# Four instead of three seven-product couples in nine of eleven gate-and-up groups, two low parts a group on GpSimd

## The chip, the cores and the metric

One core of one Trainium2 chip runs the whole program; the other cores are idle. The metric is the device time of one execution in microseconds (us). The median of the runs is compared. A smaller number is better.

## The reference

A two-layer decoder trunk over 256 tokens with a model width of 2048 and a hidden width of 5632. Layer 0 is a Conformer convolution, layer 1 a dilated attention; each is followed by a SwiGLU block. Only the two SwiGLU blocks matter here:

```python
def _swiglu(h, w_gate, w_up, w_down):
    return (jax.nn.silu(h @ w_gate) * (h @ w_up)) @ w_down
...
    for layer in range(DEPTH):
        ...                                   # convolution (layer 0) or attention (layer 1)
        h = h + _swiglu(_rmsnorm(h, ffn_norm_g[layer]), ffn_w_gate[layer],
                        ffn_w_up[layer], ffn_w_down[layer])
    return _rmsnorm(h, final_norm_g)
```

All inputs and outputs are float32.

## The kernel before

**Products.** TensorE multiplies in a rounded 32-bit form (fp32r). To keep float32 accuracy each operand is split in a high part (the value copied into fp32r) and a low part (the value minus its high part). A product of two operands is three matmuls: high by high, high by low, low by high (`nat`, lines 409, 411, 414). Activations are split once; weights are split as they arrive. A weight block is 2 x 128 rows by 512 columns, 128x1024 elements on chip. It is loaded by a DMA of SyncE's queue into a `raw` buffer (3 of them), ScalarE copies it into `whi`, VectorE subtracts into `wlo` (`split`). `whi` and `wlo` have four buffers each, and `next_block` keeps the emission two blocks ahead of the block that TensorE uses, so that a block can be prepared while TensorE is at most four blocks behind.

**Gate and up.** `ffn_hidden` runs once in each layer. It goes over 11 groups `c`; a group makes 512 gate columns and 512 up columns for all 256 tokens (two halves of 128). The 2048 input rows are 8 couples of 2 x 128 rows. A plain couple ("n" in the items string) takes one gate block and one up block, 12 matmuls of 128x512 each, together 24. A couple by seven products ("S") treats tokens x rows and rows x (gate, up) as 2 x 2 matrices and needs 7 instead of 8 products, 21 matmuls (`seven`). For that it needs sums of the activation parts, made once (`sum_up`, kept in `xsums`), and four sums of weight parts: `emit_sums` loads the four parts into one tile `four` (two DMAs of GpSimd's queue, `load_sums`), and prepares four "quarters" q = 0 to 3 with one 1024-element low part each (512 at q = 1), and with three more subtractions `less` on VectorE (line 261). Group 0 has plain couples only (the sums are made beside it); groups 1 to 10 have `"nnSnSnSn"`: two plain couples ahead, then S and n in turn.

**End of a group.** After the last S `combine_into` (line 569, 571) puts the seven products' four extra PSUM banks together: one ScalarE copy and four VectorE additions into `work`. `hidden` then adds the group's own banks (line 713), ScalarE makes the silu (717), VectorE multiplies gate and up (724). A few block steps later `turned` transposes the result on TensorE (736), and ScalarE and VectorE split it into `hid` (738, 739). PSUM has eight banks: the four that hold one group's sums of products (`cs`) are the extra banks (`ps`) of the next, and the other way round, so a group's first matmuls wait until the additions of `combine_into` have read the banks, and the first S of a group waits for the last readers of the previous group's `cs`.

**Order.** Each engine works off its own queue in order. A scheduler orders instructions; `in_order` pins a chosen sequence of those on one engine. `later(n, ...)` runs a piece of work after n + 1 block steps (`tick`).

Lines 229 to 276 (splitting and sums), 511 to 560 (the order of couples) and 684 to 751 (`ffn_hidden`) are the ones that the steps of the prediction touch.

Of the kernel before, what the change touches and what calls it, by code (L numbers as in the profile page):

```python
# [47 lines left out]
SUMS_FF = 3  # L48
LATE = 4
ITEMS_FF = "nnSnSnSn"  # L50
# [48 lines left out]
def trunk(ctx: ExitStack, tc: tile.TileContext, xT, xN, b2, vec, const, w1, w2, wk, wv, wq, wo, wg0, wu0, wd0, wg1, wu1, wd1, fing, out):  # L99
# [66 lines left out]
    all_sums = []  # L166

# [3 lines left out]
    def ff_items(c):  # L171
        return ITEMS_FF if c else ITEMS_FF.replace("S", "n")

    def pairs_of(items, n_sums):

        n = n_sums if "S" in items else 0
        return iter(range(n)), iter(range(n, len(items)))

    def plan_two(a, b, items, n_sums, n_rest):
# [4 lines left out]
        ahead = [next(plain) for _ in range(2)]  # L184
        blocks.extend((*w, k, GKV) for w in ab for k in ahead)
        for item in items[2:len(items) - n_rest]:
            if item == "S":
                k = next(sums)
                blocks.extend(("sums", len(all_sums), q, GKV) for q in range(4))
                all_sums.append((a, b, k))  # L190
            else:
                k = next(plain)
                blocks.extend((*w, k, GKV) for w in ab)
# [42 lines left out]
    def load_sums(n):  # L236

        a, b, k = all_sums[n]
        src = [w[c, k].rearrange("p (k n) -> p k n", k=GKV) for w, c in (a, b)]
        nc.gpsimd.dma_start(places[0][:, 0:4:3, :], src[0])  # L240
        nc.gpsimd.dma_start(places[0][:, 1:3, :], src[1])  # L241

    def load_first_sums(w, *here):

        places[:] = here
        load_sums(next(n for n, s in enumerate(all_sums) if s[0][0] is w))

    def split(hi, lo, raw):
        with in_order("ACT") as made:
            made.append(nc.scalar.copy(hi, raw))  # L250
        with in_order("DVE") as made:
            made.append(nc.vector.tensor_tensor(out=lo, in0=raw, in1=hi.bitcast(F32), op=ALU.subtract))  # L252

    def emit_sums(n, q, _):

        hi, lo = (wp.tile([P, GKV, NBV], F32R, name=n, bufs=AHEAD + 2) for n in ("whi", "wlo"))
        four, t13, t24 = places
# [20 lines left out]
    def emit_block():  # L278
# [22 lines left out]
        for s in range(0, gk, step):  # L301
# [5 lines left out]
            if natural:  # L307
                split(hi, lo, raw)
# [179 lines left out]
    def sum_up(sums, u, two, h, d, order=None):  # L488
# [4 lines left out]
        hi, lo = (sums[u][:, :, i, :] for i in range(2))  # L493

# [10 lines left out]
        with order("ACT") as made:  # L505
            made.append(nc.scalar.copy(hi, d))
        op(lo, d, hi.bitcast(F32), ALU.subtract)
# [3 lines left out]
    def two_blocks(a, b, items, n_sums, n_rest, act, sums, cs, sum_banks, combine):  # L511
# [34 lines left out]
        for n, item in enumerate(body):  # L546
# [8 lines left out]
            else:  # L555
                k = next(u_plain)
                for i in range(2):
                    plain(i, k, n == len(body) - 1 and not n_rest)
# [7 lines left out]
    def combine_into(q, ps):  # L566

        p1, p5, p6, p7 = ps
        nc.scalar.copy(q[0][0], p1)
        for o, p, i in ((q[0][1], p6, q[0][0]), (q[1][0], p7, q[0][1]), (q[1][1], p5, q[1][0]), (q[0][1], p5, q[0][1])):  # L570
            nc.vector.tensor_tensor(out=o, in0=p, in1=i, op=ALU.add)
# [112 lines left out]
    def ffn_hidden(ff, scratch, wg, wu, x, norm, by_tokens, first):  # L684
# [3 lines left out]
        hid.add(new_x(ff, "hid", FT - LATE), FT - LATE)  # L688
        rooms = ff.tile([P, 2, 2, NBV], F32, name="rooms", tag="late")
        sums = places_of(ff.tile([P, SUMS_FF, 4, 2, P], F32R, name="xsums", tag="t8"), SUMS_FF)  # L690
        later(2, lambda: norm.rstd_nat(bank2))
        for k in range(SUMS_FF):
            later(3 + 3 * k, lambda k=k: sum_up(sums, k, x[:, 2 * k:2 * k + 2, :, :], room("sq"), room("sq")))
# [14 lines left out]
        def hidden(c, cs, summed):  # L708
            if summed:
# [4 lines left out]
            for t in range(2):  # L714
                g, r = q[t][0], norm.rn[:, t:t + 1]
                with in_order("ACT") as made:
                    made.append(nc.scalar.activation(g, g if summed else cs[t][0], AF.Silu, scale=r))
                silu.append(made[-1].ins)

            def product():  # L720
                for t in range(2):
                    (g, u), r = q[t], norm.rn[:, t:t + 1]
                    with in_order("DVE") as made:
                        made.append(nc.vector.scalar_tensor_tensor(out=u, in0=u if summed else cs[t][1], scalar=r, in1=g, op0=ALU.mult, op1=ALU.mult))

            product()

        def turned(c, cs):

            if c == F // NBV - 1:  # L730
                hid.add(ff.tile([P, LATE, 2, S], F32R, name="hid2", tag="late"), LATE)
# [9 lines left out]
        for c in range(F // NBV):  # L741
# [3 lines left out]
            two_blocks((wg, c), (wu, c), items, SUMS_FF, 0, x, sums, cs, ps_set,  # L745
                       lambda ps: combine_into(q, ps))
# [507 lines left out]
```

## Time and profile before

| what | value |
|---|---|
| median of 3 runs | 2116.52 us (2116.48 to 2118.3) |
| the profiled execution | 2117.25 us, span 2115.4 us, granted clock 0.997 |
| TensorE matmul busy | 2094.6 us, 99% |
| VectorE busy | 1791.9 us, 85% |
| ScalarE busy | 1188.0 us, 56% |
| GpSimd busy | 345.0 us, 16% |
| DMA moved | 418.99 MB, mean 198 GB/s |

The span is the time from the first to the last instruction of the core. The matmul busy share counts pipelined instructions with modelled ends, so that 99% says that TensorE nearly always had a matmul under way, not that no cycle was lost. The two `ffn_hidden` stages lie at about 321 to 790 us and 1405 to 1874 us of the span.

### The profile page before, as it was taken

The page shows a single profiled execution, that of the slowest core. Times are in us where ns is not written, and L with a number is a line of the kernel's source. Part 1 is how long each engine was busy: PE and PEld are TensorE (multiplying, and loading weights), DVE is VectorE, ACT ScalarE, POOL GpSimd, SP SyncE. Part 2 cuts the span into 40 slices and gives each one's busy share as a digit, 9 for nine tenths or more (in the row PEclk, how much of TensorE's full clock was granted, in tenths as well). Part 3 has the DMA queues.
Part 4 walks back from the last instruction along what each step waited for, and adds up shares of the span by engine and source line. Part 5 has one row for each costly group of instructions (what it writes and reads, how often), then busy time and mean ns, then how long its engine had stood idle before and what let it go on. Part 6 is the DMA issues. An engine that isn't in the chain of part 4 may idle for free.

```text
span 2115.4 us, 28273 instructions
## 1 busy us (share of the span) xinstructions
PE 2094.6 (99%) x10171; PEld 1764.9 (83%) x10171; DVE 1791.9 (85%) x2465; ACT 1188.0 (56%) x1575; POOL 345.0 (16%) x349
## 2 busy tenths in 40 slices
PE   9999899999999999999999999999999999999998
PEld 8999788888888888888888888888888888888886
DVE  6888987998998998868896687787998999888877
ACT  6666556555555555555654566565555555555454
POOL 4999100000000000000000100000000000000200
PEclk9999999999999999999999999999999999999999
DMA  8575457555655566565656644565555565666664
GB/s 284 185 189 162 143 173 235 190 196 193 208 199 185 200 204 238 191 218 191 224 192 193 217 158 159 203 209 190 209 189 192 205 201 192 205 219 215 208 210 150
DMA packets 120508, 418.99 MB, mean 198 GB/s; under 512 B 13104, under 2 KB 18224, under 8 KB 120112
## 3 DMA queue, kind: packets, MB, share of 16 engines
q1 hardware_dynamic: 84384, 300.77, 42.9%
q0 software_dynamic: 35264, 115.36, 16.1%
q8 instruction: 79, 1.29, 0.2%
q10 hardware_dynamic: 720, 1.07, 0.1%
q14 instruction: 61, 0.50, 0.1%
HBM read 408.76 MB, written 8.39 MB: 197 GB/s over the span
## 4 chain that ended last, share of the span: by engine, by line
PE 94%; DVE 2%; DMA 1%; ACT 1%; issue 1%; SPq 0%; POOL 0%; ACTq 0%; DVEq 0%; POOLq 0%
PE pp L409 12%; PE pp L411 12%; PE pp L414 12%; PE aux L409 10%; PE aux L414 10%; PE aux L411 10%; PE pp L400 8%; PE pp L359 6%; PE pp L363 3%; PE b L409 3%; PE b L411 3%; PE b L414 3%; DVE wlo L252 1%; DVE aux L831 0%; PE pp L736 0%
## 5 line engine op out<-in xcount | busy, mean ns | idle before, releaser
L252 DVE TENSOR_TENSOR wlo<-raw,whi 128x1024 fp32r<-128x1024 f32 x383 | 458.9, 1229 | 99.6 <-ACT whi L250 81.5
L250 ACT CAST whi<-raw 128x1024 fp32r<-128x1024 f32 x383 | 390.9, 1049 | 236.5 <-DMA raw<-wd 76.5
L250 ACT CAST whi<-rooms 128x1024 fp32r<-128x1024 f32 (+1 forms) x140 | 144.9, 1038 | 209.2 <-DVE rooms L261 165.0
L311 ACT CAST whi<-raw 128x1024 fp32r<-128x1024 f32 (+1 forms) x162 | 166.1, 1032 | 132.8 <-PE pp L400 39.1
L313 DVE TENSOR_TENSOR wlo<-raw,whi 128x1024 fp32r<-128x1024 f32 (+1 forms) x117 | 144.2, 1252 | 66.2 <-ACT whi L311 52.7
L252 DVE TENSOR_TENSOR wlo<-rooms,whi 128x1024 fp32r<-128x1024 f32 (+1 forms) x140 | 168.4, 1203 | 12.7 <-ACT whi L250 9.3
L241 POOL DMA_DIRECT2D work<-wu x60 | 32.8, 546 | 796.2 <-DVE rooms L261 769.9
L409 PE MATMUL pp<-whi,x 128*128 128x512 f32 x513 | 150.7, 392 | 0.0
L252 DVE TENSOR_TENSOR wlo<-work,whi 128x1024 fp32r<-128x1024 f32 x120 | 114.5, 954 | 42.2 <-ACT whi L250 42.2
L414 PE MATMUL pp<-wlo,x 128*128 128x512 f32 x513 | 149.1, 389 | 0.0
L411 PE MATMUL pp<-whi,x 128*128 128x512 f32 x513 | 149.0, 389 | 0.0
L831 DVE SCALAR_TENSOR_TENSOR aux<-up,vecs,aux 128x256 f32<-128x256 f32 x350 | 140.9, 483 | 4.0 <-ACT aux L829 4.0
L250 ACT CAST whi<-work 128x1024 fp32r<-128x1024 f32 x120 | 95.4, 833 | 70.0 <-DMA work<-wg 36.7
L411 PE MATMUL aux<-whi,x 128*128 128x512 f32 x404 | 134.0, 389 | 0.0
L409 PE MATMUL aux<-whi,x 128*128 128x512 f32 x404 | 133.4, 392 | 0.0
L414 PE MATMUL aux<-wlo,x 128*128 128x512 f32 x404 | 132.5, 389 | 0.1
L409 PEld LDWEIGHTS pp<-whi,x 128*128 128x128 f32 x513 | 96.1, 188 | 22.6 <-DVE hid L739 3.0
L414 PEld LDWEIGHTS pp<-wlo,x 128*128 128x128 f32 x513 | 96.3, 188 | 20.2
L313 POOL TENSOR_TENSOR wlo<-raw,whi 128x1024 fp32r<-128x1024 f32 x45 | 109.4, 2469 | 21.2 <-ACT whi L311 21.2
L411 PEld LDWEIGHTS pp<-whi,x 128*128 128x128 f32 x513 | 96.3, 188 | 19.8
L400 PE MATMUL pp<-x,whi 128*128 128x256 f32 x600 | 111.9, 288 | 0.0
L359 PE MATMUL pp<-x,whi 128*128 128x512 f32 x448 | 109.8, 393 | 0.0
(407 smaller groups left out, 4915.3 us busy)
## 6 DMA issues: line engine op xcount, KB each, us to landing
raw<-wd SPq DMA_DIRECT2D x128, 512.0 KB, 4.4
raw<-wg SPq DMA_DIRECT2D x116, 512.0 KB, 4.0
raw<-wu SPq DMA_DIRECT2D x116, 512.0 KB, 3.9
raw<-w SPq DMA_DIRECT2D x71, 512.0 KB, 3.7
work<-wg POOLq DMA_DIRECT2D x60, 512.0 KB, 4.6
work<-wu POOLq DMA_DIRECT2D x60, 512.0 KB, 3.8
t<-wd POOLq DMA_DIRECT2D x48, 512.0 KB, 4.4
raw<-wk SPq DMA_DIRECT2D x32, 512.0 KB, 3.7
```

Source lines behind the costliest of these rows:

```text
L241: nc.gpsimd.dma_start(places[0][:, 1:3, :], src[1])
L250: made.append(nc.scalar.copy(hi, raw))
L252: made.append(nc.vector.tensor_tensor(out=lo, in0=raw, in1=hi.bitcast(F32), op=ALU.subtract))
L311: nc.scalar.copy(hi[:, part, :], raw[:, part, :])
L313: made = eng.tensor_tensor(out=lo[:, part, :], in0=raw[:, part, :], in1=hi[:, part, :].bitcast(F32), op=ALU.subtract)
L359: nc.tensor.matmul(bk[:, m, :, :], hi, x[:, k, :, :], start=k == 0, stop=k == kt_n - 1 and turned, skip_group_check=True)
L363: nc.tensor.matmul(bk[:, m, 0, :], lo, x[:, k, 0, :], start=False, stop=k == kt_n - 1 and not turned, skip_group_check=True)
L400: nc.tensor.matmul(bks[u][:, m, :], a[:, j, m * P:(m + 1) * P], b, start=kt == 0 and m == 0 and i == 0, stop=kt == DT - 1 and i == len(pas ...
L409: nc.tensor.matmul(o, xs[0], hi, start=start, stop=False, skip_group_check=True)
L411: nc.tensor.matmul(o, xs[1], hi, start=False, stop=False, skip_group_check=True)
L414: nc.tensor.matmul(o, xs[0], lo, start=False, stop=stop and last[id(o)] == n, skip_group_check=True)
L831: nc.vector.scalar_tensor_tensor(out=acc[i % 2], in0=win, scalar=w, in1=acc[i % 2], op0=ALU.mult, op1=ALU.add)
```

## The change

Groups 1 to 9 of each layer take `"nnS0S1S0S1"`: four couples by seven products and four plain ones. Two plain couples open the group; the other two are cut into their gate half ("0") and up half ("1"), one after each S. Group 10 keeps `"nnSnSnSn"`, group 0 stays plain.

The sums of the fourth couple (couple 3) need a place: three of their four parts go into quarters of the activation tile `x` that no later matmul reads (rows 0, 2 and 4, second token half: a couple by seven products reads the first half of its first row tile and both of its second), the fourth into a small tile `apart`. The tile `hid` becomes shorter by four, and the space is a second `four` tile, `early`, until group 9's hidden values move in. So the weights for the sums alternate between two tiles, and the next load of a tile is issued right after q = 1, when its last reader is done, and no longer after q = 3.

In groups 2 to 10 the low parts of blocks 1 and 2 of the group (the second gate block, the first up block) are made by GpSimd, not VectorE. `split` sets them aside; `beside` issues them with a dependency on a VectorE instruction: the first waits for the last VectorE low part ahead of `combine_into`, the second for the last addition of `combine_into`. `hidden` emits block 2 a step earlier than before, `turned` runs 3 block steps after the group's end instead of 6, the silu writes back into PSUM (`cs[t][0]`) and the product reads it there.

```diff
-SUMS_FF = 3
+SUMS_FF = 4
-ITEMS_FF = "nnSnSnSn"
+ITEMS_FF = "nnS0S1S0S1"
+LAST_FF = "nnSnSnSn"
...
     def ff_items(c):
-        return ITEMS_FF if c else ITEMS_FF.replace("S", "n")
+        return "n" * (D // NBV * 2) if not c else LAST_FF if c == F // NBV - 1 else ITEMS_FF
...
-            plan_two((wg, c), (wu, c), ff_items(c), ff_items(1).count("S"), 0)
+            plan_two((wg, c), (wu, c), ff_items(c), ff_items(c).count("S"), 0, (1, 2) if c > 1 else (), (0, 1) if c < F // NBV - 1 else (0,))
...
+    def beside():
+
+        def low(hi, lo, raw):
+            with in_order("POOL") as made:
+                made.append(nc.gpsimd.tensor_tensor(out=lo, in0=raw, in1=hi.bitcast(F32), op=ALU.subtract))
+            tc.add_manual_dep(made[-1].ins, (anchor.pop() if anchor else last_split["DVE"]).name,
+                              mybir.DependencyInfo(mybir.DependencyClass.Sync, mybir.DependencyReason.DATA), reason="beside")
+
+        while waiting:
+            low(*waiting.pop())
+
+    def split(hi, lo, raw, here=True):
         with in_order("ACT") as made:
             made.append(nc.scalar.copy(hi, raw))
+        if not here:
+            waiting.append((hi, lo, raw))
+            if anchor:
+                beside()
+            return
         with in_order("DVE") as made:
             made.append(nc.vector.tensor_tensor(out=lo, in0=raw, in1=hi.bitcast(F32), op=ALU.subtract))
...
             less(t24[:, 0, :], four[:, 2, :], t13[:, 0, :])
             less(t24[:, 1, :], four[:, 3, :], t24[:, 0, :])
+            load_sums(n + 1, w, slot)
         elif q == 2:
             split(hi, lo, t13)
         else:
             split(hi, lo, t24)
-            if n + 1 < len(all_sums) and all_sums[n + 1][0][0] is all_sums[n][0][0]:
-                load_sums(n + 1)
...
-        hid.add(new_x(ff, "hid", FT - LATE), FT - LATE)
+        hid.add(new_x(ff, "hid", FT - 2 * LATE), FT - 2 * LATE)
+        early = ff.tile([P, 4, NBV], F32, name="early", tag="early")
...
+        apart = Joined()
+        apart.add(x.parts[0][0][:, 0:2 * SUMS_FF - 2:2, :, P:S], SUMS_FF - 1)
+        apart.add(sp.tile([P, 1, 2, P], F32R, name="apart", tag="sqacc", bufs=1), 1)
+        sums.append(apart)
...
         def hidden(c, cs, summed):
+            if 0 < c < F // NBV - 1:
+                emit_block()
+                beside()
...
-                    made.append(nc.scalar.activation(g, g if summed else cs[t][0], AF.Silu, scale=r))
+                    made.append(nc.scalar.activation(cs[t][0] if summed else g, g if summed else cs[t][0], AF.Silu, scale=r))
...
+        def combined(c, ps):
+
+            if c < F // NBV - 1:
+                anchor[:] = [last_split["DVE"]]
+            combine_into(q, ps, in_order)
...
-            later(5, lambda c=c, cs=cs: turned(c, cs))
+            later(2, lambda c=c, cs=cs: turned(c, cs))
```

How the instructions move is shown at three places. The first is VectorE at the end of a middle group, before the change: the names are tiles, `wlo<-raw,whi` is a low part, line 571 the additions of `combine_into`, 713 those of `hidden`, 724 the product, and the rows below 724 are the next group's plain blocks and its first S.

```order
L252 TENSOR_TENSOR wlo<-raw,whi 128x1024 x3
L571 TENSOR_TENSOR work<-pp,work 128x512 x4
L252 TENSOR_TENSOR wlo<-raw,whi 128x1024
L713 TENSOR_TENSOR work<-aux,work 128x512 x3
L713 TENSOR_TENSOR work<-b,work 128x512
L724 SCALAR_TENSOR_TENSOR work<-work,rstdn_61 128x512 x2
L252 TENSOR_TENSOR wlo<-raw,whi 128x1024 x2
L252 TENSOR_TENSOR wlo<-work,whi 128x1024
```

And the same place after the change, where the lines are 608, 758 and 769, low parts are line 282 and the subtractions of weight parts line 293.

```order
L282 TENSOR_TENSOR wlo<-raw,whi 128x1024 x2
L608 TENSOR_TENSOR work<-pp,work 128x512 x4
L758 TENSOR_TENSOR work<-aux,work 128x512 x3
L758 TENSOR_TENSOR work<-b,work 128x512
L769 SCALAR_TENSOR_TENSOR work<-work,rstdn_61,aux 128x512 x2
L282 TENSOR_TENSOR wlo<-raw,whi 128x1024
L282 TENSOR_TENSOR wlo<-early,whi 128x1024
L293 TENSOR_TENSOR rooms<-early 128x1024
L282 TENSOR_TENSOR wlo<-early,whi 128x512
L293 TENSOR_TENSOR rooms<-early,rooms 128x512 x2
L790 TENSOR_TENSOR hid<-aux,hid 128x2x256
L790 TENSOR_TENSOR hid<-b,hid 128x2x256
```

Two low parts have left VectorE between the last S and the first S of the next group; the ten instructions with a PSUM operand (608, 758, 769) now stand in one run, and `hid` (790) is split inside the first S.

The second place is GpSimd's queue around the end of a group after the change: line 266 are the two low parts, 251 and 252 the loads of weights for the sums.

```order
L252 DMA early<-wu 128x1024
L251 DMA early<-wg 128x2x512
L252 DMA work<-wu 128x1024
L251 DMA work<-wg 128x2x512
L266 TENSOR_TENSOR wlo<-raw,whi 128x1024 x2
L252 DMA early<-wu 128x1024
L251 DMA early<-wg 128x2x512
```

Before, this queue held only the loads (lines 240, 241, one pair for each S). Now both loads for the next group stand ahead of the two low parts, and the next pair, which waits for VectorE in the next group's first S, stands behind them.

The third place is TensorE near the start of a group. Line 736 are the transposes of the previous group's hidden values, 409, 411 and 414 the three matmuls of a product; `xsums` marks a quarter of a seven-product couple. Before:

```order
L409 MATMUL pp<-whi,xsums 128x512
L411 MATMUL pp<-whi,xsums 128x512
L414 MATMUL pp<-wlo,xsums 128x512
L736 MATMUL aux<-cst,work 128x128 x4
L736 MATMUL b<-cst,work 128x128 x4
L409 MATMUL aux<-whi,xsums 128x512
L411 MATMUL aux<-whi,xsums 128x512
```

After the change the transposes are line 787, the three matmuls 440, 442 and 445:

```order
L445 MATMUL b<-wlo,x 128x512
L445 MATMUL aux<-wlo,x 128x512
L445 MATMUL b<-wlo,x 128x512
L787 MATMUL pp<-cst,work 128x128 x8
L440 MATMUL aux<-whi,x 128x512
L440 MATMUL b<-whi,x 128x512
```

The transposes have moved from the middle of the group's first seven-product couple to behind its third plain block.

More of the change, by code (lines that the diff above doesn't have):

```diff
@@ L184, in plan_two @@
         ahead = [next(plain) for _ in range(2)]
+        aside.update(len(blocks) + k for k in outer)
         blocks.extend((*w, k, GKV) for w in ab for k in ahead)
@@ L307, in emit_block @@
             if natural:
-                split(hi, lo, raw)
+                split(hi, lo, raw, i not in aside)
                 continue
@@ L504, in sum_up @@
         op(d[:, 3, :], a12, d[:, 1, :], ALU.subtract)
-        with order("ACT") as made:
-            made.append(nc.scalar.copy(hi, d))
-        op(lo, d, hi.bitcast(F32), ALU.subtract)
+        at = 0
+        for tile, n in sums[u].parts if isinstance(sums[u], Joined) else [(sums[u], 4)]:
+            hi, lo = (tile[:, :, i, :] for i in range(2))
+            with order("ACT") as made:
+                made.append(nc.scalar.copy(hi, d[:, at:at + n, :]))
+            op(lo, d[:, at:at + n, :], hi.bitcast(F32), ALU.subtract)
+            at += n
     n_used = [0]
```

70 lines of the change are left out of this document (43 added, 27 removed).

## The prediction

> **What bounds the kernel now.** I read the page first (busy shares, chain), then the stretches of two groups, then TensorE's rows and waits, and at last VectorE's rows of one group.
>
> ```profile
> PE 2094.6 (99%) x10171; PEld 1764.9 (83%) x10171; DVE 1791.9 (85%) x2465; ACT 1188.0 (56%) x1575; POOL 345.0 (16%) x349
> PE 94%; DVE 2%; DMA 1%; ACT 1%; issue 1%; SPq 0%; POOL 0%; ACTq 0%; DVEq 0%; POOLq 0%
> core 0: us, PE busy (x) PEld busy (x) DVE busy (x) ACT busy (x) POOL busy (x), PEclk, DMA share, GB/s
> 550.31:635.44 85.13, 85.13 (x384) 70.20 (x383) 77.54 (x87) 47.15 (x54) 7.53 (x12) 1.00 0.59 198
> 1591.84:1676.95 85.11, 85.11 (x383) 70.21 (x383) 77.42 (x87) 47.03 (x54) 7.53 (x12) 1.00 0.57 198
> ```
>
> TensorE carries 94% of the chain of waits. The two stretches are two groups each, one stretch in either layer: TensorE busy throughout at full clock, VectorE busy 77.5 of 85.1 us. So a group takes 42.56 us, and VectorE, with 3.8 us idle in it, is the next limit. ScalarE, GpSimd and the DMA are far from full. The question is whether TensorE stays the bound when its time shrinks and VectorE's grows.
>
> ```profile
> 574.80 1.07 PE L409 MATMUL pp<-whi,xrest 128*128 128x512 f32 x4
> 577.52 1.07 PE L409 MATMUL aux<-whi,x 128*128 128x512 f32 x4
> 589.77 1.03 PE L736 MATMUL pp<-cst,work 128*128 128x128 f32 x8
> 590.87 0.40 PE L411 MATMUL aux<-whi,x 128*128 128x512 f32 x1
> PEld pp L409 <- DVE hid L739: 3.0, 10, 0.3
> PEld aux L409 <- DVE hid L739: 2.9, 10, 0.3
> ```
>
> A block of 12 matmuls starts at 574.80, the next at 577.52: 2.72 us, 0.227 us a matmul. The eight transposes start at 589.77, and after them and one matmul (0.227) the next starts at 590.87: 0.87 us. A group of five plain and three seven-product couples has 5 x 24 + 3 x 21 = 183 matmuls: 41.49 + 0.87 = 42.36. So 0.2 us of 42.56 is lost in each group, and the two wait rows name the place: the first seven-product couple waits 0.3 us, 20 times, until VectorE has split the previous group's hidden values.
>
> **The matmuls.** Nine groups of each layer replace one plain couple by seven products: 3 matmuls less in 18 groups, 54 x 0.227 = 12.2 us. A plain couple that is cut in halves costs TensorE nothing. A group now needs 180 x 0.2267 + 0.87 = 41.68 us. If the 0.2 us also goes, a group saves 0.88, in all 15.9 us.
>
> **VectorE's load.** The rows of one group, in order of time:
>
> ```profile
> 605.96 1.23 DVE L252 TENSOR_TENSOR wlo<-work,whi 128x1024 fp32r<-128x1024 f32 x1 [1.21 <-ACT whi L250]
> 607.10 1.22 DVE L261 TENSOR_TENSOR rooms<-work 128x1024 f32<-128x1024 f32 x1
> 608.24 0.69 DVE L252 TENSOR_TENSOR wlo<-work,whi 128x512 fp32r<-128x512 f32 x1
> 608.84 1.41 DVE L261 TENSOR_TENSOR rooms<-work,rooms 128x512 f32<-128x512 f32 x2
> 610.16 2.50 DVE L252 TENSOR_TENSOR wlo<-rooms,whi 128x1024 fp32r<-128x1024 f32 x2
> 612.59 3.49 DVE L252 TENSOR_TENSOR wlo<-raw,whi 128x1024 fp32r<-128x1024 f32 x3
> 615.99 2.73 DVE L571 TENSOR_TENSOR work<-pp,work 128x512 f32<-128x512 f32 x4
> 618.64 1.22 DVE L252 TENSOR_TENSOR wlo<-raw,whi 128x1024 fp32r<-128x1024 f32 x1
> 619.77 1.88 DVE L713 TENSOR_TENSOR work<-aux,work 128x512 f32<-128x512 f32 x3
> 622.17 1.41 DVE L724 SCALAR_TENSOR_TENSOR work<-work,rstdn 128x512 f32<-128x512 f32 x2
> 623.49 2.36 DVE L252 TENSOR_TENSOR wlo<-raw,whi 128x1024 fp32r<-128x1024 f32 x2
> 635.48 0.68 DVE L739 TENSOR_TENSOR hid<-aux,hid 128x512 fp32r<-128x512 f32 x1
> 636.08 0.68 DVE L739 TENSOR_TENSOR hid<-b,hid 128x512 fp32r<-128x512 f32 x1
> ```
>
> From start to start: a seven-product couple 6.63 (605.96 to 612.59), three plain low parts 3.40, so 1.13 each, the four additions of the combination 2.65, the group's own four 2.40, the two products 1.32, the two splits of hidden values 0.60 each. Before: 10 x 1.13 + 3 x 6.63 + 2.65 + 2.40 + 1.32 + 1.20 = 38.8, which is the 77.5 of two groups. After: one couple more (+6.63), two plain blocks fewer (-2.27), two low parts to GpSimd (-2.27): 40.9 of 41.68. VectorE is 98% full and has 0.8 us left. Its products read one operand in PSUM instead of SBUF; group 0 already does that, at the duration of the others:
>
> ```profile
> L724 DVE SCALAR_TENSOR_TENSOR work<-work,rstdn x40: 740/744/749, 410.2 to 1878.6; 128x512 f32<-128x512 f32 x40
> L724 DVE SCALAR_TENSOR_TENSOR work<-aux,rstdn,work x1: 751/751/751, 364.7 to 364.7; 128x512 f32<-128x512 f32 x1
> ```
>
> **Where VectorE must not be late.** Count from the first matmul of a group. TensorE: three plain blocks to 8.16, transposes to 9.03, the fourth block to 11.75, first seven-product couple to 16.51, then half a plain couple and a couple by turns, 7.48 each, the last couple ending at 38.96, the last half at 41.68. VectorE may be at most four blocks ahead (four buffers): the last quarter's low part of the first couple cannot start before the fourth plain block is done at 11.75 and ScalarE has copied its high part, 1.05 us (the row below), so it ends at about 14.1. It is needed in the third pass of that quarter, at 16.0: 1.9 us of lead. From there VectorE takes 1.13 + 6.63 = 7.77 for what TensorE does in 7.48 and loses 0.29 each time; at the fourth couple the lead is 1.0. At 37.4 it goes on to two plain low parts and the combination's first addition, which ends at 40.4; the next group's first matmul needs its bank at 41.68. That cover was two blocks (5.44) and is now one (2.72), and 1.2 us of it are left. The next group's first couple needs the hidden values split at 11.75: VectorE ends the combination at 42.4, adds and products at 46.1, which is 4.4 in the next group, one low part and half of the couple's work (5.35 together) bring it to 9.8, the first split to 10.4. The lead is 1.3, so the old 0.2 us should go. All leads are near one microsecond: thin, but on TensorE's side.
>
> **GpSimd's low parts.** The rows beside which they are priced: GpSimd's own low parts in the first stage, VectorE beside it with one operand in PSUM, the same form with GpSimd idle, and VectorE with both operands in SBUF.
>
> ```profile
> L313 POOL TENSOR_TENSOR wlo<-raw,whi x45: 2360/2392/4020, 29.8 to 209.7; 128x1024 fp32r<-128x1024 f32 x45
> 83.64 7.06 POOL L313 TENSOR_TENSOR wlo<-raw,whi 128x1024 fp32r<-128x1024 f32 x3
> 85.59 0.41 DVE L872 TENSOR_TENSOR cT<-aux,prod 128x256 f32<-128x256 f32 x1
> L1083 DVE TENSOR_TENSOR o<-aux,o x16: 415/418/425, 1230.9 to 1326.0; 128x256 fp32r<-128x256 f32 x16
> 1123.25 1.29 POOL L1112 TENSOR_TENSOR kT<-t,rstd 128x512 f32<-128x512 f32 x1 [33.34 <-DVE t L423]
> 1123.41 2.20 DVE L313 TENSOR_TENSOR wlo<-raw,whi 128x1024 fp32r<-128x1024 f32 x1 [0.26 <-ACT whi L311]
> 1202.38 3.49 DVE L313 TENSOR_TENSOR wlo<-raw,whi 128x1024 fp32r<-128x1024 f32 x3
> 1202.54 4.47 POOL L1112 TENSOR_TENSOR kT<-t,rstd 128x512 f32<-128x512 f32 x1 [11.28 <-DVE t L423]
> DMA to landing us min/median/max: 3.4/3.7/5.7
> 571.77 1.05 ACT L250 CAST whi<-raw 128x1024 fp32r<-128x1024 f32 x1
> ```
>
> A low part takes GpSimd 2.39 us. VectorE's addition with one operand in PSUM takes 0.41 beside it and 0.42 alone: no cost. With both operands in SBUF the two shut each other out: VectorE's 1.22 becomes 2.20 when GpSimd began first (1123), and GpSimd's 1.29 becomes 4.47, to the end of three VectorE low parts, when VectorE began first (1202). The Trainium skill ("SBUF — State Buffer", section "SBUF: two separate sides") has this as an exclusive lock on a shared port pair, held for a whole instruction by whichever starts first, for VectorE with two SBUF inputs; by that rule the 36 low parts that moved save VectorE nothing unless its own instructions beside them read PSUM. The two rows above agree with it.
>
> Here they do read PSUM. The first GpSimd low part starts when VectorE turns to the combination (39.7) and ends at 42.1, inside its 2.65 us. The second needs its raw block: the buffer comes free with the last half's low part at 38.6, the DMA lands 3.7 later at 42.3 (the landing row is of the raw blocks from 430 to 760 us), ScalarE's copy ends at 43.4, GpSimd at 45.8, just ahead of VectorE's return to SBUF at 46.1. I take zero for both. The bounds: at the slowest landing, 5.7, GpSimd ends at 47.8 and VectorE is held 1.7 us in that group; below zero nothing, since VectorE has no more to lose than the two low parts already counted. TensorE needs the second low part at 5.44 + 1.81 in the next group, 48.9, so its own lead is 3 us.
>
> The loads on GpSimd's queue stand ahead of the low parts and wait for VectorE's subtractions in the fourth couple, which are done by 35, so they hold up nothing; behind them waits the load for the next group's first couple's tile, which has a whole group. 36 DMAs more, the same bytes. In group 0 the fourth sum adds about eight VectorE instructions beside 16 low parts (18 us of 43): hidden. Group 1 keeps four low parts on VectorE and has no combination ahead of it; it comes out with less load than the others.
>
> **The sum.** -12.2 (matmuls) - 1.8 (half of the lost 3.6) + 0.6 (my allowance for two starting groups in which leads are thin, between 0 and 2) = -13.4. The profiled execution takes 2117.25 (span 2115.4), so 2103.9; the median of the runs is 0.73 lower, and I forecast against it: 2116.5 - 13.4 = 2103. Between all of the 15.9 and a new wait of 0.2 us in each group (8.6 gained) it is 2100.6 to 2108.
>
> **Rivals.**
> (1) VectorE becomes the bound. An extra of e us in each group beyond the 0.8 left lengthens 18 groups by e - 0.8. The idle that the waits don't explain and a landing later than 3.7 would make it: with e = 1.2 it takes back 7 us, 2108 to 2111; with e = 1.68 nothing is left of the gain. For it: 98% load, leads of one microsecond. Against: VectorE's durations repeat within 2% (740 to 749 ns).
> (2) On the other side, slower: GpSimd comes too late. If the second low part's copy is ready only after VectorE has gone back to SBUF (46.1 in place of 43.4, a landing of 6.4), it is shut out through VectorE's run of 5.35 us, as in the row at 1202, starts at 9.8 in the next group, ends at 12.2, and TensorE, which needed it at 7.25, waits 4.9. In all 18 groups 18 x (4.9 - 0.88) = +72, 2189; in four of them it already takes back 20 us. It decides from a landing of 6.4; the longest there was 5.7. If GpSimd instead wins each time, VectorE is held for both low parts, 4.78 us, and 18 x (4.78 - 0.8) - 15.9 is 56 us slower. The lock of the page named above is this mechanism.
> (3) The change frees TensorE and nothing follows: the 0.68 us come back as a wait at the group's start, where the combination's cover is halved. From a combination later than 1.2 us it decides; at 1.9 us late the time is 2116.
>
> **How the numbers follow.** TensorE stays the bound 0.67; rival 1 0.15 (mostly still faster); rival 2 0.09; rival 3 0.05; something not seen 0.04. About 4 us, 0.2%, is what a measurement of this kernel can tell from no change. Faster 0.81, within 0.2% 0.08, slower 0.11. The range 2099 to 2112 takes in the likeliest case and rival 1 up to e = 1.2; the rest is left out.
>
> **What would show it.** Two middle groups take 83.4 to 83.8 us instead of 85.1; VectorE is busy about 81 in them; the two GpSimd low parts last 2.4 each and lie beside additions with PSUM operands; the waits of weight loads on hidden values are gone. It is wrong if TensorE has waits on `wlo` or on the combination in every group, or if GpSimd's low parts last over 3 us.

## The result and the profile after

| what | before | after |
|---|---|---|
| median of 4 runs | 2116.5 us (2116.01 to 2118.3) | 2101.38 us (2100.08 to 2102.02) |
| profiled execution, span | 2115.4 us | 2098.3 us |
| two middle groups | 85.13 us | 83.42 us |

The ratio is 0.9926, with a 95% interval of 0.9909 to 0.9943: 15.1 us faster. Forecast were 2103, likeliest 2100.6 to 2108, in a stated range of 2099 to 2112. The profiled execution gained 17.1 us of span, 1.6 of it already ahead of the first gate and up stage (the first matmul of its first group at 317.35 against 318.95), which no part of the change touches; 15.5 are left for the rest.

The same views as before, of the changed kernel: the page's busy shares and chain, then two groups in each layer (columns as in the prediction's stretches: length, then busy time of PE, PEld, DVE, ACT, POOL).

```profile
PE 2077.5 (99%) x10117; PEld 1755.3 (84%) x10117; DVE 1829.5 (87%) x2533; ACT 1218.1 (58%) x1615; POOL 456.1 (22%) x421
PE 94%; DVE 2%; DMA 2%; ACT 1%; issue 1%; SPq 0%; POOL 0%; ACTq 0%; DVEq 0%; POOLq 0%
571.77:655.19 83.42, 83.42 (x378) 69.23 (x377) 81.01 (x93) 50.21 (x58) 19.82 (x21) 1.00 0.60 201
1573.56:1656.98 83.42, 83.42 (x377) 69.23 (x377) 81.02 (x93) 50.20 (x59) 19.84 (x20) 1.00 0.63 202
```

TensorE is busy through both stretches and carries the same 94% of the chain. A group takes 41.71 us, where 180 matmuls and the transposes come to 41.68: nothing is lost any more. 18 groups times 42.56 - 41.71 = 0.85 is 15.3 us, against the measured 15.1.

What is left of VectorE's idle time in the first of these stretches (us in total, times, longest):

```profile
DVE wlo L282 <- ACT whi L275: 0.8, 2, 0.5
DVE wlo L282 <- PE pp L445: 0.6, 1, 0.6
DVE work L769 <- ACT pp L762: 0.3, 1, 0.3
```

1.7 us in two groups, 0.85 a group. The other gaps on VectorE are too short for a row of their own; with them counted as work, its work is 41.71 - 0.85 = 40.86 us a group. Without them, by the busy column (81.01 for two groups), it is 40.5, and 1.2 us a group are idle, against 3.8 before. Of the waits of weight loads on hidden values, ten and ten times 0.3 us before, no row is left.

The end of the two kinds of group, and of the group at 450 us (GpSimd's rows, then VectorE's; the idle time before a row and what ended it in brackets), the product's and the GpSimd rows of the whole run, and the landing of the raw blocks from 430 to 740 us:

```profile
569.93 2.41 POOL L266 TENSOR_TENSOR wlo<-raw,whi 128x1024 fp32r<-128x1024 f32 x1 [3.86 <-DVE wlo L282]
573.20 2.41 POOL L266 TENSOR_TENSOR wlo<-raw,whi 128x1024 fp32r<-128x1024 f32 x1 [0.86 <-ACT whi L275]
615.14 2.41 POOL L266 TENSOR_TENSOR wlo<-raw,whi 128x1024 fp32r<-128x1024 f32 x1 [0.39 <-ACT whi L275]
448.43 2.43 POOL L266 TENSOR_TENSOR wlo<-raw,whi 128x1024 fp32r<-128x1024 f32 x1 [0.51 <-DVE work L758]
572.23 2.47 DVE L758 TENSOR_TENSOR work<-pp,work 128x512 f32<-128x512 f32 x4
575.00 1.41 DVE L769 SCALAR_TENSOR_TENSOR work<-work,rstdn,pp 128x512 f32<-128x512 f32 x2 [0.29 <-ACT pp L762]
576.32 1.22 DVE L282 TENSOR_TENSOR wlo<-raw,whi 128x1024 fp32r<-128x1024 f32 x1
617.65 1.22 DVE L282 TENSOR_TENSOR wlo<-raw,whi 128x1024 fp32r<-128x1024 f32 x1
450.82 1.22 DVE L282 TENSOR_TENSOR wlo<-raw,whi 128x1024 fp32r<-128x1024 f32 x1
L769 DVE SCALAR_TENSOR_TENSOR work<-work,rstdn,aux x20: 737/743/747, 449.5 to 1818.2; 128x512 f32<-128x512 f32 x20
L266 POOL TENSOR_TENSOR wlo<-raw,whi x36: 2393/2411/2426, 403.4 to 1816.2; 128x1024 fp32r<-128x1024 f32 x36
DMA to landing us min/median/max: 3.3/3.6/6.2
```

The 36 low parts on GpSimd take 2.39 to 2.43 us, VectorE's additions and products beside them take what they always took. The second low part ends at 575.61 in the one kind of group, beside a product that reads PSUM, and at 617.55 in the other, 0.1 us ahead of VectorE's return to SBUF at 617.65. The margin is thin: over the 18 groups the end lies between 0.7 us ahead of VectorE's return and 0.04 us behind it (the group at 450 us), where VectorE's row still takes 1.22. In the 18 groups the second low part waits 0.15 to 1.46 us after the first, in most of them for the high part that follows the landing; that wait now stands on GpSimd.

### The profile page after: what moved, and what is told of

The parts are those of the page before. It is cut to its first block, busy times and chain, and to the rows that moved or that the text cites. A ratio compares the mean times of both kernels' runs of the same rounds, so it can differ in the third digit from the quotient of the medians.

```text
span 2098.3 us, 28482 instructions
## 1 busy us (share of the span) xinstructions
PE 2077.5 (99%) x10117; PEld 1755.3 (84%) x10117; DVE 1829.5 (87%) x2533; ACT 1218.1 (58%) x1615; POOL 456.1 (22%) x421
## 4 chain that ended last, share of the span: by engine, by line
PE 94%; DVE 2%; DMA 2%; ACT 1%; issue 1%; SPq 0%; POOL 0%; ACTq 0%; DVEq 0%; POOLq 0%
PE pp L440 12%; PE pp L442 12%; PE pp L445 12%; PE aux L440 10%; PE aux L445 10%; PE aux L442 10%; PE pp L431 8%; PE pp L390 5%; PE pp L394 3%; PE b L440 3%; PE b L442 3%; PE b L445 3%; DVE wlo L282 1%; PE pp L787 0%; DMA raw<-wd 0%
## 5 line engine op out<-in xcount | busy, mean ns | idle before, releaser
L275 ACT CAST whi<-raw 128x1024 fp32r<-128x1024 f32 x347 | 359.0, 1050 | 203.9 <-DMA raw<-wd 64.8
L282 DVE TENSOR_TENSOR wlo<-raw,whi 128x1024 fp32r<-128x1024 f32 x311 | 376.5, 1233 | 88.9 <-ACT whi L275 69.1
L275 ACT CAST whi<-rooms 128x1024 fp32r<-128x1024 f32 (+1 forms) x176 | 182.7, 1040 | 270.3 <-DVE rooms L293 229.3
L282 DVE TENSOR_TENSOR wlo<-rooms,whi 128x1024 fp32r<-128x1024 f32 (+1 forms) x176 | 211.5, 1206 | 11.7 <-ACT whi L275 8.0
L344 POOL TENSOR_TENSOR wlo<-raw,whi 128x1024 fp32r<-128x1024 f32 x45 | 109.5, 2473 | 22.4 <-ACT whi L342 22.4
L442 PEld LDWEIGHTS pp<-whi,x 128*128 128x128 f32 x495 | 92.9, 188 | 19.5
L266 POOL TENSOR_TENSOR wlo<-raw,whi 128x1024 fp32r<-128x1024 f32 x36 | 86.8, 2411 | 94.7 <-ACT whi L275 53.6
L440 PEld LDWEIGHTS pp<-whi,x 128*128 128x128 f32 x495 | 92.0, 188 | 18.3
L275 ACT CAST whi<-t 128x1024 fp32r<-128x1024 f32 (+1 forms) x72 | 64.2, 909 | 60.3 <-DVE t L293 35.8
L390 PEld LDWEIGHTS pp<-x,whi 128*128 128x128 f32 x448 | 82.3, 188 | 15.9
```

What stands on the lines that cost most here:

```text
L266: made.append(nc.gpsimd.tensor_tensor(out=lo, in0=raw, in1=hi.bitcast(F32), op=ALU.subtract))
L344: made = eng.tensor_tensor(out=lo[:, part, :], in0=raw[:, part, :], in1=hi[:, part, :].bitcast(F32), op=ALU.subtract)
L390: nc.tensor.matmul(bk[:, m, :, :], hi, x[:, k, :, :], start=k == 0, stop=k == kt_n - 1 and turned, skip_group_check=True)
L440: nc.tensor.matmul(o, xs[0], hi, start=start, stop=False, skip_group_check=True)
L442: nc.tensor.matmul(o, xs[1], hi, start=False, stop=False, skip_group_check=True)
```

## The experiments

Theory A is that of the prediction: TensorE bounds with 41.68 us a group, VectorE has 0.8 us of room, and GpSimd's low parts are free because they lie beside instructions with a PSUM operand. Where theory A missed, theory A2 was formed: VectorE's group is its work plus the waits that stand on its queue, and these waits are no room. In these sums VectorE's work is the 40.86 us above, short gaps included. The kernels, each with the kernel before on the same chip:

| kernel | us | ratio to before, 95% | two groups, us |
|---|---|---|---|
| e1_all_on_vector | 2131.61 | 1.0054 to 1.0082 | 86.96 |
| e2_one_on_gpsimd | 2126.11 | 1.0032 to 1.0058 | 86.78 |
| e3_no_fourth_couple | 2123.37 | 1.0022 to 1.0047 | 85.90 |
| e4_late_transposes | 2111.83 | 0.9969 to 0.9986 | 84.49 |
| e5_second_only | 2109.54 | 0.9956 to 0.9980 | 84.40 |
| e6_three_couples_split_end | 2114.20 | 0.9980 to 0.9998 | 84.78 |
| e7_fourth_raw_buffer | 2127.30 | 1.0036 to 1.0061 | 85.8 |
| e8_before_early_transposes | 2112.88 | 0.9973 to 0.9990 | 84.78 |
| e9_gpsimd_midgroup | 2164.79 | 1.0218 to 1.0246 | 90.91 |
| e10_product_in_sbuf | 2109.59 | 0.9959 to 0.9983 | 84.16 |
| e11_last_group_too | 2112.91 | 0.9977 to 0.9995 | as after |

The last column is the mean over four groups near 490 to 670 us (two groups in e9), from one product to the next but one.

**No low part on GpSimd, and one.**

```diff
-... ff_items(c).count("S"), 0, (1, 2) if c > 1 else (), ...   # after
+... ff_items(c).count("S"), 0, (), ...                        # e1_all_on_vector
+... ff_items(c).count("S"), 0, (1,) if c > 1 else (), ...     # e2_one_on_gpsimd
+... ff_items(c).count("S"), 0, (2,) if c > 1 else (), ...     # e5_second_only
```

> The changed kernel with all low parts on VectorE again (none on GpSimd). Theory A (TensorE sets the time as long as VectorE's work of a group, 40.9 us, stays under TensorE's 41.7): VectorE's work rises by 2 x 1.13 to 43.1, VectorE becomes the bound, 18 groups x 1.4 = 26 us more than the changed kernel, about 2127, which is 10 slower than the kernel before. Two middle groups take 86.3 us. Rival B (VectorE has more slack than its rows say, because of the four buffers and GpSimd's part is not needed): within 4 us of 2101.

> The changed kernel with one low part a group on GpSimd (block 1) and the other on VectorE. Theory A: VectorE's work is 40.9 + 1.13 = 42.0 against 41.7 of TensorE, 0.3 too much in each of 18 groups: 5 us more, 2106 to 2109 with the waits that cannot be hidden. Two middle groups take 84.0 to 84.4. Rival B (slack is larger): 2101. Rival C (the cost of VectorE's work is not its sum but a late combination): already half of the 26 us of the kernel without GpSimd, 2114.

> One low part a group on GpSimd again, but the second one (that of block 2, whose raw values land last before the combination) in place of the first. Theory A2 (in the run with the first one alone VectorE lost twice: 1.2 us of work came back, and its low part of block 2 waited 0.76 to 0.88 us behind the landing, ahead of the combination): here that wait sits on GpSimd, VectorE has 42.0 us of work and a wait of 0.3 a group, so a group takes 42.3 and the whole 2101 + 18 x 0.6 = 2112 (2109 to 2115); two groups 84.5 to 85. Rival (only the number of low parts taken off VectorE counts): 2126, two groups 86.8, as with the first alone.

The stretches of two groups, e1's first, then e2's, then e5's:

```profile
497.39:584.01 86.62, 85.71 (x378) 68.56 (x377) 85.45 (x96) 49.94 (x59) 10.04 (x16) 1.00 0.58 195
584.01:671.31 87.30, 86.37 (x380) 69.11 (x379) 85.61 (x97) 49.94 (x59) 10.06 (x16) 1.00 0.57 192
497.30:583.48 86.18, 85.74 (x377) 68.45 (x376) 83.36 (x94) 49.95 (x59) 14.96 (x18) 1.00 0.58 195
583.48:670.86 87.38, 86.52 (x381) 69.16 (x380) 83.36 (x94) 49.94 (x59) 14.97 (x18) 1.00 0.58 193
494.84:579.25 84.41, 84.41 (x378) 68.86 (x377) 83.19 (x94) 50.03 (x59) 15.17 (x18) 1.00 0.61 200
```

Without GpSimd (e1) the change loses: VectorE's work is 40.86 + 2 x 1.13 = 43.1 a group, its waits in the four groups come to 1.4 us (0.35 a group), and the group takes 43.48. Theory A had the direction and 25.6 of the 30.2 us; the 0.35 was taken as room and is none.

With the first low part alone (e2) theory A missed by 17 us, and the rival of that run too. VectorE's work is then 42.0, but a group takes 43.4. The rows of VectorE and ScalarE in e2 at the end of a group, and VectorE's waits for high parts in the four groups:

```profile
579.58 1.22 DVE L282 TENSOR_TENSOR wlo<-raw,whi 128x1024 fp32r<-128x1024 f32 x1 [0.88 <-ACT whi L275]
580.72 2.48 DVE L758 TENSOR_TENSOR work<-pp,work 128x512 f32<-128x512 f32 x4
578.49 1.05 ACT L275 CAST whi<-raw 128x1024 fp32r<-128x1024 f32 x1 [2.65 <-DMA raw<-wu]
DVE wlo L282 <- ACT whi L275: 4.5, 4, 1.6
```

The second block is loaded only when a low part of VectorE has freed a raw buffer (574.9), and lands at 578.4; ScalarE's copy follows, and VectorE, in order, stands 0.88 us ahead of its four additions (L758) until the copy is there. In all it waits 4.5 us and 0.6 for silu in four groups, 1.3 a group, and 42.0 + 1.3 = 43.3. So the second low part does two things on GpSimd: it takes 1.13 us of work off VectorE, and it takes the wait behind the landing off VectorE's queue.

e5 tells this from a mere count of low parts: the same number, one, but the second. Expected 2112, measured 2109.5; a count of low parts gave 2126. VectorE's only wait there is 0.3 for silu in three groups of four, 0.2 a group, and 42.0 + 0.2 = 42.2 is the group. Of the two low parts the late one is worth 22 us (e1 to e5), the early one 8 us (e5 to after); taken in the other order, the early one is worth 5.5 us (e1 to e2) and the late one 24.7 (e2 to after).

**Three couples, in two orders.**

```diff
-ITEMS_FF = "nnS0S1S0S1"
+ITEMS_FF = "nnSnSnSn"      # e3_no_fourth_couple
+ITEMS_FF = "nnnSnS0S1"     # e6_three_couples_split_end
```

> All of the change but the fourth couple by seven products (groups 1 to 10 with three, in the old order; two low parts a group on GpSimd, two tiles for the loads, early transposes stay). Theory A: the matmuls of before, 183 a group, without the 0.2 us wait for hidden values: 42.36 a group, 20 x 0.2 = 4 us less than before, 2112.5; two middle groups 84.7. Rival D (a good part of the gain is VectorE's relief and the earlier loads, not the matmuls): under 2108.

> Three couples by seven products in place of four, with the order nnnSnS0S1: the group still ends in a sums couple and half a couple. Theory A2 (with three couples and a whole plain couple at the end the three raw buffers were the limit: the first GpSimd low part began 4.6 us ahead of the product's end against 6.5): with the end as in the changed kernel that goes, TensorE bounds with 183 matmuls, 183 x 0.2267 + 0.87 = 42.36 us a group, so 2101 + 18 x 0.65 = 2113 (2110 to 2116), two groups 84.7. Rival (two low parts on GpSimd cost this much wherever the couple count is three): 2123, two groups 85.9.

e3 was to lose the matmuls' 11 us and lost 22: it is slower than before. VectorE has room there (73 us busy of 85.9). The chain of waits of e3 at a group's end, word for word from 571.84 on:

```profile
571.84 1.24 DVE wlo L282
...
573.09 3.59 DMA raw<-wg
...
576.78 1.06 ACT whi L275
...
577.97 2.58 POOL wlo L266
...
580.57 3.57 DMA raw<-wu
...
584.22 1.06 ACT whi L275
...
585.30 0.06 DVE wlo L282
```

A raw buffer is freed, loaded, copied, subtracted on GpSimd (2.58), freed, loaded and copied again: 13.5 us, twice a landing of 3.6, with VectorE idle for 2.7 us at its end. Behind its last sums e3 has two raw blocks of the whole plain couple and then the next group's. With three buffers, GpSimd's first block is the fourth of this run: it has to wait for a buffer and a load, and the next load but one waits for GpSimd. In e6 the three couples stay, but the group ends as in the changed kernel, in a sums couple and half a couple, and the whole couple moves to the head of the group, which now opens with three plain couples. There GpSimd's first block is the third of the run. The two groups of each, e3 first, and e6's two low parts on GpSimd at a group's end:

```profile
495.27:581.21 85.94, 85.14 (x384) 70.20 (x383) 73.04 (x84) 47.97 (x54) 18.10 (x17) 1.00 0.56 196
493.06:577.84 84.78, 84.78 (x384) 70.36 (x383) 73.32 (x83) 48.13 (x55) 17.33 (x17) 1.00 0.62 199
572.75 2.40 POOL L266 TENSOR_TENSOR wlo<-raw,whi 128x1024 fp32r<-128x1024 f32 x1 [3.87 <-PE pp L445]
576.17 2.41 POOL L266 TENSOR_TENSOR wlo<-raw,whi 128x1024 fp32r<-128x1024 f32 x1 [1.01 <-ACT whi L275]
```

84.78 is 2 x 42.39, TensorE's 183 matmuls and transposes (42.36) and nothing else. 2114.2 was measured, 2113 expected; the rival's 2123 is out. The number of raw blocks in a row is not what counts: e6 has seven of them where e3 has six. In e6 GpSimd begins at 572.75, 5.1 us ahead of the product (577.84); in e3 at 577.97, 3.2 us ahead of it (581.21). So the order of the couples is a part of the change with a price of its own: 9 us where GpSimd makes low parts. How much of it is the end of the group, and how much its head, was not separated. From e6 to after the fourth couple comes in and the order changes once more; TensorE is busy throughout in both, and 84.78 - 83.42 = 1.36 for two groups, 0.68 a group, is the time of three matmuls: 12.2 us in 18.

**A fourth raw buffer.** It was to show that the chain over the buffers is the cause in e3.

```diff
-            raw = wp.tile(shape, F32, name="raw", bufs=RAW)
+            raw = fourth[0] if i in spare else wp.tile(shape, F32, name="raw", bufs=RAW)
...
+        fourth[:] = [early[:, 0:2, :]]
```

> The kernel with three couples and the whole plain couple at the end (2123 measured), in which the first GpSimd block of groups 2 to 8 of each stage is loaded into a fourth buffer (the tile early, free since the quarters then use one place only). Theory A2: the chain over the three raw buffers opens, those 14 groups go from 42.95 to 42.4, so 2123 - 8 = 2115 (2113 to 2118), and VectorE's wait of 2.7 to 3.4 us for the high part behind the product goes or halves. Rival (the chain is set by GpSimd's two low parts in a row, 4.9 us, not by when the buffers come free): 2121 to 2125.

The trace has no row of ScalarE that reads `early`: the name `spare` also stood for another tile of the program, and no block went into the fourth buffer. The kernel differs from e3 only in one place for the quarters instead of two, and its 2127.3 (85.8 for two groups) says nothing on the chain. That the three buffers are the limit in e3 is read from its chain and agrees with e6, but it is not shown: a fourth buffer itself was not tried.

**The transposes, earlier and later.**

```diff
-            later(5, lambda c=c, cs=cs: turned(c, cs))
+            later(2, lambda c=c, cs=cs: turned(c, cs))    # in before: e8_before_early_transposes
...
-            later(2, lambda c=c, cs=cs: turned(c, cs))
+            later(5, lambda c=c, cs=cs: turned(c, cs))    # in after: e4_late_transposes
```

> The kernel before, with the transposes of the hidden values three blocks earlier, later(2) in place of later(5), and nothing else. Theory A: the 0.2 us a group that the weight loads of the first seven-product couple waited for hidden values goes, two groups from 85.13 to 84.7, 2116.5 - 3.6 = 2113. Rival (the wait comes back elsewhere, since VectorE then does the split of the hidden values ahead of the quarters of the first couple): 2116 to 2118, two groups 85.1.

> The changed kernel with the transposes of hidden values at their old place, six block steps after the group's end. Theory A: the wait of 0.2 to 0.3 us comes back in each group, 4 to 6 us more, 2105 to 2107; two middle groups 83.9. Rival E (the transposes' place is without effect, the wait went because of the other order of couples): 2101.

Two groups of e8, two of e4, e4's waits of weight loads in the whole run, and a row of VectorE in e4:

```profile
491.94:576.72 84.78, 84.78 (x384) 70.35 (x383) 77.74 (x88) 48.14 (x55) 7.55 (x12) 1.00 0.57 198
494.76:579.25 84.49, 84.48 (x378) 68.92 (x377) 81.26 (x92) 50.15 (x59) 19.80 (x21) 1.00 0.59 200
PEld pp L440 <- ACT whi L275: 8.4, 20, 0.9
PEld pp L445 <- DVE wlo L282: 3.8, 10, 0.5
PEld pp L440 <- DVE hid L790: 2.3, 8, 0.3
592.61 1.22 DVE L282 TENSOR_TENSOR wlo<-work,whi 128x1024 fp32r<-128x1024 f32 x1 [1.32 <-ACT whi L275]
```

In the kernel before, the earlier transposes alone give 85.13 - 84.78 = 0.35 for two groups, 3.2 us in 18 groups; the median moved 3.8. That is the whole 0.2 us a group that the first seven-product couple had waited for hidden values. With 3.2 from this line and 12.2 from the fourth couple the change's 15.3 is complete. And e8, which makes no low part on GpSimd in these groups, takes the same 84.78 as e6: with three couples GpSimd's help brings nothing, it is there to carry the fourth. In the changed kernel the same line is worth 10.4 us, not 4 to 6. VectorE is idle for only 1.2 us a group there instead of 3.8. In e4 it splits the hidden values at 590.01, after the whole of the first couple's preparation, and then stands 1.32 us until ScalarE has copied the second couple's first high part (592.61). So high and low parts come late as well: the weight loads wait 8.4 + 3.8 us for them, waits of which the changed kernel has no row in the middle groups.

**GpSimd beside SBUF work.**

```diff
-... (1, 2) if c > 1 else (), ...
+... (8, 18) if c > 1 else (), ...
...
-            waiting.append((hi, lo, raw))
-            if anchor:
-                beside()
+            with in_order("POOL") as made:
+                made.append(nc.gpsimd.tensor_tensor(out=lo, in0=raw, in1=hi.bitcast(F32), op=ALU.subtract))
```

> Two low parts a group on GpSimd as in the changed kernel, but those of two plain half blocks in mid-group (indices 8 and 18 of the group), issued as soon as their high part is there, so that VectorE does low parts and quarters with both inputs in SBUF beside them. Theory A (GpSimd and VectorE shut each other out where both read SBUF twice, as in the early stage before: 1.22 to 2.20 on VectorE, up to 4.47 on GpSimd): a low part of GpSimd stretches to about 4 to 5 us or VectorE is held, some 3.5 us a low part and 7 a group with VectorE at its bound, less the 0.85 of room: 2101 + 18 x 6 = 2210 (2150 to 2240). Rival B (no such shutting out; only the place of the wait on the landing counts): GpSimd rows stay at 2.4 us and VectorE's at 1.22, VectorE waits 0.8 to 1.2 us a group behind the landing again, 2103 to 2112.

```profile
501.98:592.89 90.91, 87.10 (x378) 68.29 (x377) 87.04 (x93) 50.01 (x59) 19.91 (x20) 1.00 0.56 186
512.16 2.44 POOL L278 TENSOR_TENSOR wlo<-raw,whi 128x1024 fp32r<-128x1024 f32 x1 [1.16 <-ACT whi L275]
513.01 2.67 DVE L281 TENSOR_TENSOR wlo<-work,whi 128x1024 fp32r<-128x1024 f32 x1 [0.68 <-ACT whi L275]
L278 POOL TENSOR_TENSOR wlo<-raw,whi x34: 2423/2434/2493, 421.2 to 1893.3; 128x1024 fp32r<-128x1024 f32 x34
```

Again two low parts a group on GpSimd (one in the last group of a layer, where the second of the two places is a block of sums), and 63 us slower. VectorE's low part starts at 513.01 and takes 2.67 instead of 1.22: it ends 1.08 us after GpSimd's (514.60), so it stood until GpSimd was through; all 34 of them take 2.66 to 2.68. GpSimd's own rows keep 2.42 to 2.49. So the shutting out is there, and rival B (2103 to 2112) is out; but its price was overestimated (2210 expected, 2150 at the least). GpSimd never lost here, since each time it started only some 0.2 us before VectorE's run ahead of it ended, and VectorE lost 1.45 us a low part, 2.9 a group, where 7 had been supposed. The other 0.8 of the 3.74 that a group grew are VectorE's waits for high parts.

**The product back in SBUF.**

```diff
-... activation(cs[t][0] if summed else g, g if summed else cs[t][0], AF.Silu, scale=r))
+... activation(g, g if summed else cs[t][0], AF.Silu, scale=r))
-... in1=cs[t][0] if summed else g, op0=ALU.mult, op1=ALU.mult))
+... in1=g, op0=ALU.mult, op1=ALU.mult))
```

> The changed kernel with silu written to SBUF again, so that the product reads both its inputs there, while the end of GpSimd's second low part overlaps its first 0.6 us in every second group (573.20 + 2.41 against 575.00). Theory A: VectorE or GpSimd loses at most those 0.6 us, within VectorE's room of 0.85 a group: 2101 to 2104, the product's rows at 0.74 to 1.4 us. Rival: GpSimd does not get through until VectorE's run of SBUF work ends, the third raw buffer comes free late and the next group's first blocks wait: 2 us a group, 2137.

```profile
533.39 2.41 POOL L266 TENSOR_TENSOR wlo<-raw,whi 128x1024 fp32r<-128x1024 f32 x1 [0.17 <-ACT whi L275]
534.81 2.20 DVE L769 SCALAR_TENSOR_TENSOR work<-work,rstdn 128x512 f32<-128x512 f32 x2
576.54 2.20 DVE L769 SCALAR_TENSOR_TENSOR work<-work,rstdn 128x512 f32<-128x512 f32 x2
PEld pp L440 <- DVE hid L790: 1.7, 2, 1.0
```

The two products take 2.20 instead of 1.40: the first stands until GpSimd ends at 535.80. So it is in all 18 groups: the first product ends 0.55 us after GpSimd and loses 0.8 to 1.7 us. The pair lost 0.8 us in the two groups shown, and what follows it comes late: weight loads wait for hidden values again, 1.7 us in four groups (the last line), and two groups take 84.16 instead of 83.42. 8.2 us in all, where 0 to 3 were expected: the 0.85 of room does not cover a delay at this place; the transposes and the hidden values follow the product. The rival's 2137 is out.

**Four couples in the last group too.**

```diff
-        return "n" * (D // NBV * 2) if not c else LAST_FF if c == F // NBV - 1 else ITEMS_FF
+        return "n" * (D // NBV * 2) if not c else ITEMS_FF
```

> The changed kernel with four seven-product couples in the last group of each stage too. Theory A (TensorE is the bound, 0.65 to 0.68 us for a couple): 2 groups, 1.4 us less, 2100.0 (2098.5 to 2101.5), which the measurement can hardly tell from 2101.4; the pitch of the last groups shows it, 0.7 us shorter. Rival (the last group's low parts are followed by the down stage's loads and VectorE is short there): 2102 to 2104.

```profile
754.01 1.57 ACT L275 CAST whi<-work 128x1024 fp32r<-128x1024 f32 x2 [1.53 <-DMA work<-wg]
764.29 1.57 ACT L275 CAST whi<-work 128x1024 fp32r<-128x1024 f32 x2 [2.79 <-DMA work<-wg]
774.62 1.57 ACT L275 CAST whi<-work 128x1024 fp32r<-128x1024 f32 x2 [2.85 <-DMA work<-wg]
```

11.5 us slower than the changed kernel, where theory A had 1.4 us faster and the rival 1 to 3 slower. In the last group the tile `early` already holds hidden values, so its couples have one place for their four parts, and the high parts of three of its couples wait 1.5 to 2.9 us for the transfer, 7.2 us together. The group lost as much (its product comes at 791.38 instead of 784.02, with the one before it at 742.28 instead of 742.13); the second stage's lost 7.5, and about 3 us come back in the stages behind them. The changed kernel is the best of all versions run.

## Why the prediction was right, and by how much each step was off

- *The matmuls, 12.2 us.* Measured 12.2: 84.78 to 83.42 between e6 and after, which differ in the fourth couple and the order of the couples, with TensorE busy throughout in both.
- *The lost 0.2 us a group.* The prediction held that it would go, and entered only half, -1.8. This is the first mis-sized term: it went in every group, 3.2 us by e8's stretches, with the earlier transposes as its cause.
- *The allowance of +0.6 for starting groups.* Nothing of it was seen (from the first matmul of group 0 to the first that reads hidden values the two stages gained 15.7 us, no less than the 15.3 of the 18 groups); this is the second. The two terms together are 2.0 us; 1.6 lie between 2103 and the measured 2101.4.
- *VectorE's load, 40.9 of 41.68, 0.8 left.* By the busy column, to which the 38.8 for the kernel before corresponds, 40.5 were measured and 1.2 left: the load was put 0.4 too high. The 0.8 agrees with the 0.85 of waits that have a row. That this is room was wrong in part: e1 and e2 show that waits of 0.35 and 1.3 us a group stand on VectorE's queue when its work grows, and e10 that a delay of 0.8 at the product reaches TensorE.
- *GpSimd's low parts at no cost.* Right. 2.41 against the 2.39 used, the second ending from 0.7 us ahead of VectorE's return to 0.04 behind it (0.3 ahead had been worked out). The landing of the raw blocks had 6.2 as its longest, above the 5.7 taken from before. But that was another block: the second low part's own block took 3.4 to 3.9 us in all 18 groups, far from the 6.4 from which rival 2 decides. No GpSimd row grew.
- *The price of rival 2.* The mechanism is real, as e9 and e10 show, and the Trainium skill ("SBUF — State Buffer", section "SBUF: two separate sides") has it as an exclusive lock for the whole instruction, with which these rows agree. Its size in the kernel, 4.78 us a group with GpSimd winning each time, was above the 2.9 of e9: VectorE was held there for what was left of GpSimd's instruction, not for all of it. The other direction, GpSimd shut out through a run of VectorE's, from which rival 2 has its 72 us, came up in none of these runs; only the row at 1202 of the kernel before shows it.
- *Rivals 1 and 3.* Neither came. With VectorE's work 1.1 us larger, rival 1 is e5 (8 us lost); with 2.3 more, e1 (slower than before). No weight load waits for the combination.
- *What the prediction did not see.* The end of the group in half a couple was priced at nothing ("a plain couple that is cut in halves costs TensorE nothing") and looked at only as a shorter cover for the combination. By e3 and e6 the order of the couples, of which this end is a part, is worth 9 us with three raw buffers and two low parts on GpSimd. That the forecast came out in spite of it is no merit of its reasoning on this point: the change happened to bring the order that works. And the second place for the weight parts was not priced at all; e11 puts it at 7 us for the last group.

## What to carry to other kernels

When an engine in order stands at 98%, do not count its idle time as room: ask which wait each part of it is, and whether that wait stays on the engine's queue; of two equal instructions, the one that waits behind a late transfer was worth 22 to 25 us when it was moved, the other 5.5 to 8. Work for GpSimd belonged beside VectorE instructions that read PSUM (e9, with it elsewhere, took 63 us more), and it was worth writing an intermediate to PSUM (the silu, 8 us) to make that so. A change of order at a stage's seam is to be followed through the buffer ring, from the freeing engine to the landing to the next use, before it is priced at nothing.

## What the runs showed of the hardware

With both operands in SBUF, a VectorE instruction that comes after a GpSimd one has begun gets through only when that one has ended: 2.67 us instead of 1.22 for a 1024-element low part (e9), 2.20 instead of 1.40 for two products (e10), with GpSimd's 2.4 us unchanged. That a product with one operand in PSUM is not held at all (737 to 747 ns in the 20 rows shown) was counted on; that 36 low parts would repeat within 33 ns beside it was not.
